# A hybrid decoder step: the first stage by pairs of token tiles

## The chip, the core and the metric

The kernel runs on one core of one Trainium2 chip. The metric is device time in microseconds (us), the median of several runs. A core has a matrix engine (TensorE, PE in the rows, with its weight loads as PEld), a vector engine (VectorE, DVE), an activation engine (ScalarE, ACT), a general engine (GpSimd, POOL) and a queue engine (SyncE, SP) that issues most transfers. Each works through its own instructions in order and waits on semaphores of the others.

## The reference, cut to what matters

One layer is computed for 1024 prompt tokens and for 8 single decode tokens. The first stage, which the change is about, is this:

```python
h = rms_norm(x, norm_g)                      # x: (1024 + 8) x 1024
proj = h @ w_in                              # w_in: 1024 x 3864
b_gate, c_gate, conv_in, z_conv, q, kv, gate_logits, z_attn = split(proj)
q = rope(rms_norm(q, q_gain), pos) * HEAD_DIM ** -0.5      # 8 heads of 64
kv = kv.reshape(bsz, t, 3, 2, 2, 64)         # branch, key or value, head, 64
k = rope(rms_norm(kv[:, :, :, 0], k_gain), pos)
kv_cmp = einsum('bcrjgd,rjde->bcjge', blocks_of_32(kv[branch 0]) + cmp_pe, cmp_w)
```

The second stage is attention in three branches (compressed, selected, window), a short convolution, gates and the output projection; the kernel's diff leaves it alone but for one address.

## The kernel before, in words

All products are made in float32r as three matmuls (high x high, high x low, low x high), so every operand is split: a copy in float32r is the high part, the difference is the low part. For weights this is done by `w_loader`: `fetch` loads a raw piece of two 128-row slices through SP, `split` makes `wh` on ACT and `wl` on POOL.

There are nine token tiles: eight of 128 prompt tokens and one of the 8 decode tokens. In the first stage (`phase0`) a tile of x is loaded (`x_load`, L373), squared and summed on ACT (L382), its root taken in four small DVE steps (`rsqrt`, L194 to L197), scaled on DVE (L384), transposed on PE (L392, `turn_x`) and written as `hH` (ACT) and `hL` (DVE). Then five passes run over the nine tiles, each with 24 matmuls a tile (`tok_mm`, L208 to L210): the keys and values of the compressed, the selected and the window branch, and two halves of Q. Behind each tile follow its norm and rotation on DVE (`norm_rope`, L259 to L275), the output rows and, for keys, doubled rows (`twice`, tile `kd`) that PE transposes one or two tiles later (`cmp_transposes` L408, `k_finish` L489). Such later steps stand in a list `posts`; `posted(n)` runs those that are due, and `posted(9)` flushes it at the end of a pass. Between the selected and the window pass the compression is made (L599).

Beside `phase0` runs `chan_stream`, which makes the same projection with channels on the partitions (`chan_mm`, L223 to L225), in chunks of up to 384 tokens; a first part of it (`z_part`, twelve chunks) is woven into the five passes by `merge`, by weights. The framework lists the instructions in this order, and may move one that it expects to be ready ahead of one that it does not; the order on each engine is then fixed.

PSUM has eight banks: three for matmul results (`mm`), three for transposes (`tp`), two (`cc`) for warm-up matmuls and compression. x has three buffers. `mixC` and `mixA`, outputs of a later stage, lend their memory: `mixC` holds the rope tables, the norm gain as 128 equal rows (`gbc`), and a scratch row. The second rope table's slot is that of `gbc`.

Of the kernel before, what the change touches and what calls it, by code (L numbers as in the profile page):

```python
# [16 lines left out]
D = 1024  # L17
# [43 lines left out]
def hymba_step_kernel(ctx, tc, io):  # L61
    nc = tc.nc
    WARM = 24
# [60 lines left out]
    kv1p = left.enter_context(pool("kv1"))  # L124
    K, V = {}, {}

    K[1] = kv1p.tile([128, 2, 32 + SEQ], F32R, name="k1")
    kpc = K[1][:, :, 0:32]
    KOFF = {1: 32, 2: 0}
    V[1] = kv1p.tile([128, 8, 2, 128], F32R, name="v1")  # L130
# [16 lines left out]
    warm = ps.tile([128, 512], F32, name="cc", tag="cc", bufs=2)  # L147
    for _ in range(WARM):
        PE.matmul(warm[:, :256], vpc[:, 0], vpc.rearrange("p g c -> p (g c)"), start=True, stop=True)

    banks = {"mm": [(ps, "mm", 3)], "tp": [(ps, "tp", 3)], "cc": [(ps, "cc", 2)]}
# [9 lines left out]
    def w_loader(wp, n, kp, raw_bufs, hk, hl_bufs, lo_eng=POOL):  # L161


        def load(col, width):
            hs, ls, raws = [], [], []

            def fetch(i, home=wp):
                r = home.tile([128, kp, n], F32, name="wraw", bufs=raw_bufs)
# [32 lines left out]
    def tok_mm(t, w, n):  # L201

        o = bank("mm")
# [47 lines left out]
    E2 = [(DVE, DVE), (DVE, DVE), (DVE, DVE), (DVE, DVE)]  # L251

    def norm_rope(wk, src, n, t, nh, ct, sn, ea=DVE, eb=DVE):
        w = nh * 64
        sq = wk.tile([128, 256], F32, name="sq")
        ss = wk.tile([128, 8], F32, name="ss", bufs=4)
        if nh == 4:
            ACT.activation(sq[:n, :w], src, AF.Square, scale=0.125)
            DVE.tensor_reduce(ss[:n, :nh], sq[:n, :w].rearrange("p (h d) -> p h d", h=nh), axis=AX, op=OP.add)  # L259
        else:  # L260
            for h in range(nh):
                c = slice(h * 64, h * 64 + 64)
                ACT.activation(sq[:n, c], src[:, c], AF.Square, scale=0.125, accum_out=ss[:n, h:h + 1])
        r = rsqrt(wk, ss[:n, :nh], n, nh)
        qn = wk.tile([128, 4, 64], F32, name="qn")
        q = qn[:n, :nh]
        DVE.tensor_tensor(q, src.rearrange("p (h d) -> p h d", h=nh), r[:, :, None].to_broadcast([n, nh, 64]), OP.mult)
        a = wk.tile([128, 4, 64], F32, name="ra")
        b = wk.tile([128, 4, 64], F32, name="rb")
        ea.tensor_tensor(a[:n, :nh], q, ct[:n, t][:, None, :].to_broadcast([n, nh, 64]), OP.mult)  # L270
        for i in range(2):
            o, s = slice(32 * i, 32 * i + 32), slice(32 - 32 * i, 64 - 32 * i)
            eb.tensor_tensor(b[:n, :nh, o], q[:, :, s],
                               sn[:n, t, o][:, None, :].to_broadcast([n, nh, 32]), OP.mult)
        DVE.tensor_tensor(src.rearrange("p (h d) -> p h d", h=nh), a[:n, :nh], b[:n, :nh], OP.add)  # L275

    def twice(wk, rows, n):

        kd = wk.tile([128, n, 2, 64], F32, name=f"kd{n}", tag="cwr" if n == 4 else "kd2", bufs=CWR if n == 4 else 3)
        v = rows[:, :n * 64].rearrange("p (a d) -> p a d", a=n)  # L280
        copy(DVE, kd, v[:, :, None, :].to_broadcast([128, n, 2, 64]))
        return kd

    def kv_rows(wk, o, t, br, ct, sn):

        if t < 8:
            n, src = 128, o
            rows = wk.tile([128, 256], F32, name="rows", bufs=ROWS)
        else:
            n, src = 8, sum_halves(wk, o, 280 if br == 2 else 256)  # L290
            rows = srows[br] if br else wk.tile([128, 256], F32, name="rows", bufs=ROWS)[:8]
        copy(ACT, rows[:n], src[:n, :256])
        if br == 2:
            copy(ACT, gates[:n, t, :], src[:n, 256:280])
        norm_rope(wk, rows[:n, 0:128], n, t, 2, ct, sn, *E2[br])
        if t == 8:
            if br < 2:
                SP.dma_start(s_rows[br], rows)
            else:
                SP.dma_start(s_win[:, 511, :], rows)  # L300
        elif br < 2:
            SP.dma_start(p_rows[br][t * 128:(t + 1) * 128], rows)
        elif t >= 4:
            SP.dma_start(p_rows[2][(t - 4) * 128:(t - 3) * 128], rows)
        return rows, src


    LAG, DEPTH, HK, HB, XB, ZW, CWR = 1, 2, 2, 4, 3, 43.0, 1
# [6 lines left out]
    def chan_stream():  # L315
# [7 lines left out]
        for p in range(2):  # L323
            nxt[2](p)
# [31 lines left out]
    SM = 0  # L356
    ROWS = 3
    wl0 = w_loader(wk, 280, 2, 2, 1, 10)
    gbc = mCf[:, 2304:3328]

    xcs = ExitStack()
    xcp = xcs.enter_context(pool("xc"))
# [7 lines left out]
    def x_load(t):  # L370
        xts[t] = xsp.tile([128, D], F32, name="xt", bufs=XB)
# [4 lines left out]

    def x_norm(t):
# [3 lines left out]
        ss = wk.tile([128, 1], F32, name="xss", bufs=3)  # L381
        ACT.activation(junk[:n], xt, AF.Square, scale=1.0 / 32, accum_out=ss[:n])  # L382
        r = rsqrt(wk, ss[:n], n, 1)
        DVE.scalar_tensor_tensor(xt, xt, r, gbc[:n], op0=OP.mult, op1=OP.mult)  # L384
# [18 lines left out]
    def cmp_transposes(kd, t):  # L403
# [3 lines left out]
        for a in range(4):  # L407
            PE.transpose(pv[:, a], kd[:, a].rearrange("p r d -> p (r d)"), ident)  # L408
        pp = p.rearrange("p (a c r) -> p a c r", a=4, r=2)
        s = slice(t * 64, t * 64 + 64)  # L410
        for r in range(2):
            q = slice(r * 64, r * 64 + 64)
            copy(ACT, XH[q, :, s], pp[q, :, :, r])
            sub(DVE, XL[q, :, s], pp[q, :, :, r], f(XH[q, :, s]))
# [3 lines left out]
    def cw_fetch(wpool, cw, i):  # L418

        raw = wpool.tile([128, 4, 2, 64], F32, name="cwr", bufs=CWR)  # L420
# [12 lines left out]
    def small_things():  # L433

        cvr = wk.tile([20, 512], F32, name="cvr", tag="cwr", bufs=CWR)
# [3 lines left out]
        SP.dma_start(io["s_conv"].rearrange("l b r c -> (l b) r c")[:, 0, :], state_conv[:, 1, :])  # L439
        p = bank("tp")  # L440
        for i in range(4):
            PE.transpose(p[:, i * 20:i * 20 + 20], cvr[:, i * 128:(i + 1) * 128], ident[:20, :20])
        pv = p[:, :80].rearrange("p (i c) -> p i c", i=4)
        copy(DVE, cvw, pv[:, :, 0:4])
        copy(DVE, stc, pv[:, :, 4:20])

        per = wk.tile([32, 128], F32, name="per", tag="sq")
        SP.dma_start(per, io["cmp_pe"].rearrange("l r j d -> (l r) (j d)"))
        per2 = wk.tile([32, 2, 2, 64], F32, name="per2", tag="qn")
        POOL.tensor_copy(per2, per.rearrange("p (j d) -> p j d", j=2)[:, :, None, :].to_broadcast([32, 2, 2, 64]))  # L450
        p = bank("tp")
# [1073 lines left out]
```

## Time and profile before

| | us |
|---|---|
| median of three runs | 937.73 |
| lowest and highest run | 934.72, 938.48 |
| the profiled execution | 939.33 |
| its span, first to last instruction | 937.6 |

The rows below come from the profiled execution and count from the start of its span. A window's row has its bounds and length, then for each of PE, PEld, DVE, ACT and POOL the busy time with the number of instructions, then the mean granted clock of TensorE (1.00 is 2.4 GHz, 0.50 is 1.2 GHz), the busy share of the DMA engines and GB/s. A row of waits says who waited for whose instruction, the total, how often, and the longest. In a timeline the square bracket is idle time just before, with what ended it; a duration with a count covers all the instructions of the row. Durations of matmuls include the time in the pipe, so their starts tell the pace. L numbers are lines of the kernel.

### The profile page before, as it was taken

How to read it: one execution, taken by the hardware profiler on the slowest of the kernel's cores; microseconds unless marked ns; L12 is line 12 of the kernel's file. 1: busy time of each engine (PE TensorE's matmuls, PEld its weight loads, DVE VectorE, ACT ScalarE, POOL GpSimd, SP SyncE). 2: the span in 40 equal slices, each digit the busy share in tenths (PEclk: the TensorE clock that was granted, in tenths of full speed). 3: DMA queues.
4: the chain of work that ended last, by engine and by line, in shares of the span. 5: the costliest groups of instructions: out<-in, count | busy, mean ns of one | idle time of the engine just before them, and what ended most of it. 6: DMA issues, size and time to landing. Idle time of an engine off the chain costs nothing.

```text
span 937.6 us, 16976 instructions
## 1 busy us (share of the span) xinstructions
PE 873.8 (93%) x5789; PEld 783.2 (84%) x5789; DVE 619.4 (66%) x1714; ACT 556.0 (59%) x1495; POOL 404.3 (43%) x550
## 2 busy tenths in 40 slices
PE   7988999999899999999989999999679999798998
PEld 6888999999689889898979899998568888576765
DVE  5896734788655555856775686577745555877883
ACT  5764543733665655656556666576757666675761
POOL 4132340311454444444434444343455543477761
PEclk8999989999999999999999999999989999899999
DMA  7513331211011000000000100001495661857631
GB/s 246 154 57 95 95 114 35 80 57 31 6 30 34 24 23 24 23 24 23 13 12 23 24 23 1 23 2 44 127 302 182 214 214 47 314 179 226 214 102 47
DMA packets 57955, 82.24 MB, mean 88 GB/s; under 512 B 14470, under 2 KB 43086, under 8 KB 55692
## 3 DMA queue, kind: packets, MB, share of 16 engines
q1 hardware_dynamic: 50956, 47.60, 16.9%
q0 software_dynamic: 6912, 33.56, 10.6%
q8 instruction: 46, 0.75, 0.3%
q14 instruction: 41, 0.34, 0.1%
HBM read 74.24 MB, written 11.10 MB: 91 GB/s over the span
## 4 chain that ended last, share of the span: by engine, by line
PE 49%; ACT 7%; DVE 7%; POOL 3%; issue 3%; DMA 1%; ACTq 0%; DVEq 0%; POOLq 0%
PE o L880 7%; PE pt L870 5%; PE s L796 5%; PE mm L225 5%; PE mm L224 5%; PE mm L223 5%; POOL P L845 2%; ACT P L786 2%; PE mm L1407 1%; PE pt L999 1%; PE mm L1405 1%; PE mm L1406 1%; PE mm L1023 1%; ACT ph L75 1%; PE o L1278 1%
## 5 line engine op out<-in xcount | busy, mean ns | idle before, releaser
L223 PE MATMUL mm<-hH,wh 128*128 128x384 f32 (+1 forms) x480 | 157.9, 329 | 0.0
L225 PE MATMUL mm<-hH,wl 128*128 128x384 f32 (+1 forms) x480 | 155.7, 324 | 0.0
L224 PE MATMUL mm<-hL,wh 128*128 128x384 f32 (+1 forms) x480 | 155.1, 323 | 0.0
L786 ACT ACTIVATE P<-P,stat 128x640 f32<-128x640 f32 (+7 forms) x192 | 112.9, 590 | 37.4 <-DVE stat L784 36.8
L79 POOL TENSOR_TENSOR wl<-wraw,wh 128x256 fp32r<-128x256 f32 (+1 forms) x120 | 87.7, 749 | 106.2 <-ACT wh L75 96.8
L79 DVE TENSOR_TENSOR pl<-pt,ph 128x512 fp32r<-128x512 f32 (+1 forms) x164 | 102.4, 636 | 45.3 <-ACT ph L75 43.9
L75 ACT ACTIVATE ph<-pt 128x512 fp32r<-128x512 f32 (+1 forms) x164 | 88.3, 549 | 66.1 <-PE pt L870 65.5
L845 POOL TENSOR_SCALAR P<-P,stat,gates 128x640 f32<-128x640 f32 (+7 forms) x128 | 101.1, 800 | 55.8 <-DVE stat L836 52.7
L870 PE MATMUL pt<-ident,P 128*128 128x128 f32 x592 | 95.5, 278 | 6.4 <-POOL P L845 3.5
L796 PE MATMUL s<-k,q 128*128 128x320 f32 (+8 forms) x416 | 95.8, 334 | 3.7 <-DVE q L79 1.5
L208 PE MATMUL mm<-wh,hH 128*128 128x256 f32 (+1 forms) x320 | 93.5, 292 | 0.4 <-ACT hH L75 0.4
L209 PE MATMUL mm<-wl,hH 128*128 128x256 f32 (+1 forms) x320 | 93.2, 292 | 0.2
L210 PE MATMUL mm<-wh,hL 128*128 128x256 f32 (+1 forms) x320 | 93.0, 291 | 0.0
L223 PEld LDWEIGHTS mm<-hH,wh 128*128 128x128 f32 x480 | 91.9, 191 | 0.8 <-DVE mixC L693 0.6
L224 PEld LDWEIGHTS mm<-hL,wh 128*128 128x128 f32 x480 | 91.9, 191 | 0.1
L225 PEld LDWEIGHTS mm<-hH,wl 128*128 128x128 f32 x480 | 91.9, 192 | 0.1
L784 DVE CUSTOM_DVE_ANT_0 P<-s,mask 128x32 f32<-128x32 f32 (+8 forms) x160 | 70.9, 473 | 27.0 <-PE s L796 22.4
L870 PEld LDWEIGHTS pt<-ident,P 128*128 128x128 f32 x592 | 70.0, 140 | 19.9 <-POOL P L845 10.1
L880 PE MATMUL o<-ph,v 128*128 128x256 f32 x264 | 74.5, 301 | 3.6 <-ACT ph L75 3.0
L880 PE MATMUL o<-pl,v 128*128 128x256 f32 x264 | 73.3, 300 | 3.3 <-DVE pl L79 3.2
L796 PEld LDWEIGHTS s<-k,q 128*128 128x128 f32 x416 | 66.8, 190 | 8.1 <-DVE q L79 1.7
L841 POOL TENSOR_SCALAR P<-P,stat,gates 128x32 f32<-128x32 f32 x64 | 22.9, 370 | 94.4 <-DVE stat L836 76.4
(342 smaller groups left out, 2182.9 us busy)
## 6 DMA issues: line engine op xcount, KB each, us to landing
wraw<-in_w_in_dram SPq DMA_DIRECT2D x56, 256.0 KB
xt<-in_x_prompt_dram SPq DMA_DIRECT2D x8, 512.0 KB
wor<-in_w_out_dram SPq DMA_DIRECT2D x16, 256.0 KB
xr<-in_x_prompt_dram SPq DMA_DIRECT2D x16, 256.0 KB
out_y_prompt_dram<-xr SPq DMA_DIRECT2D x16, 256.0 KB
sd<-in_state_win_kv_dram SPq DMA_DIRECT2D x8, 512.0 KB
out_s_win_dram<-in_state_win_kv_dram SPq DMA_DIRECT2D x8, 511.0 KB
cwr<-in_cmp_w_dram SPq DMA_DIRECT2D x32, 64.0 KB
```

Of the source, the lines that this page charges most:

```text
L75: return ACT.activation(out, in_, AF.Copy)
L79: return eng.tensor_tensor(out, a, b, OP.subtract)
L208: PE.matmul(o[:, :n], hH[t // 3][:, k, s], wh, start=k == 0, stop=False)
L209: PE.matmul(o[:, :n], hH[t // 3][:, k, s], wl, start=False, stop=False)
L223: PE.matmul(o[:, :n], wh, hH[c][:, k], start=k == 0, stop=False)
L224: PE.matmul(o[:, :n], wh, hL[c][:, k], start=False, stop=False)
L225: PE.matmul(o[:, :n], wl, hH[c][:, k], start=False, stop=k == 7)
L786: return lambda: ACT.activation(P, P, AF.Exp, bias=stt[:, 0, c:c + 1], scale=-1.0, accum_out=stt[:, 1, c:c + 1])
L796: PE.matmul(s[:, a:b], q[:, i], k, start=first, stop=not first)
L845: POOL.tensor_scalar(P[:, i, :n], P[:, i, :n], stt[:, 2, c + i:c + i + 1], gates[:, qi, gt:gt + 1], op0=OP.mult, op1=OP.mult)
L870: PE.transpose(p[:, y * 256 + i * 128:y * 256 + i * 128 + 128], src[:, i], ident)
L880: PE.matmul(o[0][:, :256], v, X[:, y * 256:y * 256 + 256], start=br == 1 and x == 0 and y == 0 and X is h[0], stop=last and y + 1 == len(p ...
```

## The change

- Nine tiles of x have memory of their own (four in `mixA`, five in a pool) and are all loaded early. The memory of the selected branch's keys and values is taken only after that pool is closed.
- The gain is loaded as one row through ACT's queue and spread over the partitions by two matmuls into two PSUM banks (`gps`), from which x is scaled. Warm-up matmuls go from 24 to 8. The banks `cc` are gone.
- `x_stat` takes the roots of two tiles at a time; `x_norm(t + 3)` follows the matmuls of tile t, `turn_x` of tile t + 1 stands right behind the matmuls of tile t (before, that of tile t + 2).
- Two token tiles share a PSUM bank; copy, norm, rotation, value parts and doubled rows are done once for the pair. Squares of keys are summed by a DVE reduction.
- For the compressed branch the doubled rows are replaced by a regrouping of token pairs through four SBUF to SBUF DMAs, so that four transposes serve two tiles, and one ACT copy and one DVE subtraction of 128 partitions replace four of each on 64.
- Later steps wait three tiles instead of one or two, output rows are stored a tile later, and passes no longer flush the list.
- Weights: a third raw buffer, splits at tiles 2 to 6, low parts in turn on POOL and DVE, and 9 buffers for split parts instead of 10. Rope tables are made inside passes.

The diff, cut to its core:

```diff
-    WARM = 24
+    WARM = 8
...
-    banks = {"mm": [(ps, "mm", 3)], "tp": [(ps, "tp", 3)], "cc": [(ps, "cc", 2)]}
+    banks = {"mm": [(ps, "mm", 3)], "tp": [(ps, "tp", 3)]}
...
-                    sub(el, l[:, :, :width], r, f(h[:, :, :width]))
+                    sub(el[j // hk % len(el)] if isinstance(el, tuple) else el, l[:, :, :width], r, f(h[:, :, :width]))
...
-    wl0 = w_loader(wk, 280, 2, 2, 1, 10)
+    wl0 = w_loader(wk, 280, 2, 2, 1, 9)
...
+        xts[t] = mAf[:, t * D:(t + 1) * D] if t < 4 else xsp.tile([128, D], F32, name=f"xt{t}")
...
+    def x_stat(*ts):
+        n = 128 if ts[0] < 8 else 8
+        ss = wk.tile([128, 2], F32, name="xss", bufs=3)
+        for i, t in enumerate(ts):
+            ACT.activation(junk[:n], xts[t][:n], AF.Square, scale=1.0 / 32, accum_out=ss[:n, i:i + 1])
+        r = rsqrt(wk, ss[:n, :len(ts)], n, len(ts))
+        for i, t in enumerate(ts):
+            roots[t] = r[:, i:i + 1]
...
-        DVE.scalar_tensor_tensor(xt, xt, r, gbc[:n], op0=OP.mult, op1=OP.mult)
+        for c in (slice(0, 512), slice(512, D)) if t == 0 else (slice(0, D),):
+            DVE.scalar_tensor_tensor(xt[:, c], xt[:, c], r, gps[:n, c], op0=OP.mult, op1=OP.mult)
...
+    def token_pairs(rows, t):
+        pr = xsp.tile([128, 4, 2, 64], F32, name="pr", bufs=2)
+        for i in range(2):
+            for r in range(2):
+                SP.dma_start(pr[i * 64:i * 64 + 64, :, r], rows[r::2, i * 256:i * 256 + 256].rearrange("p (a d) -> p a d", a=4))
+        return pr
...
+        s = slice(t * 64, t * 64 + 128)
+        copy(ACT, XH[:, :, s], pv)
+        sub(DVE, XL[:, :, s], pv, f(XH[:, :, s]))
...
+            pair.append(tok_mm(t, w, n) if t % 2 == 0 else tok_mm(t, w, n, pair[0][:, 256:512]))
+            if t % 2:
+                o = pair[0]
+                pair[:] = [kv_room(br)]
+                copy(ACT, pair[0][1], o.rearrange("p (i j c) -> p i j c", i=2, j=2))
...
+            posts.append((lambda t=t: k_finish(br, t, kd), 3))
...
     def phase0():
+        ACT.dma_start(g1, io["norm_g"])
         x_load(0)
-        SP.dma_start(gbc, bcast_rows(io["norm_g"], D))
         SP.dma_start(idt, io["c_ident"])
+        for h in range(2):
+            PE.matmul(gps[:, h * 512:h * 512 + 512], one, g1[:, h * 512:h * 512 + 512], start=True, stop=True)
...
         for t in range(NT):
-            if t + 4 < NT:
-                x_load(t + 4)
-            if t + 2 < NT:
-                turns.append(x_norm(t + 2))
-            o = tok_mm(t, c0[0], 256)
+            o = kv_tile_mm(t, c0[0], 256, 0)
             if turns:
                 turns.pop(0)()
+            if t + 3 < NT:
+                turns.append(x_norm(t + 3))
+            if t in (0, 2):
+                x_stat(t + 4, t + 5)
+            elif t == 4:
+                x_stat(8)
             posted(1)
...
+                posts.append((lambda pr=token_pairs(rows, t - 1), t=t: cmp_transposes(pr, t - 1), 3 if t < 7 else 1))
+            if t == 5:
+                tab1 = rope_tables(io["k_gain"][0, 1], 1, 1.0)
+                small_loads()
+            if t in (2, 3, 4, 5):
+                c1[2](t - 2, ACT, EL)
...
-        posted(9)
```

## Rows read from the trace of the kernel before

**Rows 1.** The page: busy time and share of each engine

```profile
PE 873.8 (93%) x5789; PEld 783.2 (84%) x5789; DVE 619.4 (66%) x1714; ACT 556.0 (59%) x1495; POOL 404.3 (43%) x550
```

**Rows 2.** Windows: length; PE, PEld, DVE, ACT, POOL busy; clock; DMA share, GB/s

```profile
8.09:65.73 57.64, 50.28 (x349) 46.72 (x349) 48.53 (x143) 37.78 (x116) 17.13 (x20) 0.91 0.45 143
65.73:111.84 46.11, 42.31 (x319) 41.34 (x319) 32.14 (x119) 22.26 (x91) 16.23 (x23) 0.96 0.35 93
111.84:172.90 61.06, 56.70 (x404) 55.62 (x403) 31.13 (x119) 29.65 (x118) 18.98 (x28) 0.92 0.27 78
172.90:231.80 58.90, 58.90 (x478) 58.59 (x477) 48.87 (x171) 26.67 (x75) 13.49 (x20) 1.00 0.20 57
```

**Rows 3.** Waits of PE, 0 to 232 us: total, times, longest

```profile
PE tp L392 <- DVE xt L384: 5.5, 4, 1.9
PE tp L489 <- DVE kd L76: 3.7, 2, 2.0
PE tp L408 <- DVE kd L76: 3.0, 2, 1.9
PE tp L392 <- DVE rs L194: 2.0, 1, 2.0
```

**Rows 4.** Windows of a few us, columns as in the windows by pass

```profile
20.00:22.00 2.00, 1.93 (x9) 1.96 (x10) 1.30 (x3) 0.60 (x1) 0.00 (x0) 0.50 1.00 372
36.00:38.00 2.00, 1.09 (x10) 1.12 (x11) 2.00 (x12) 0.99 (x2) 0.00 (x0) 1.00 0.14 41
120.00:125.00 5.00, 5.00 (x24) 5.00 (x24) 0.86 (x1) 2.61 (x7) 3.04 (x5) 0.50 0.19 53
```

**Rows 5.** Groups on DVE by shape, 0 to 232 us: busy us, mean ns, idle before

```profile
L79 DVE TENSOR_TENSOR hL<-tp,hH 128x512 fp32r<-128x512 f32 x16 | 10.4, 686 | 2.9 <-ACT hH L75 2.8
L267 DVE TENSOR_TENSOR qn<-rows,rs 128x128 f32<-128x128 f32 x24 | 9.2, 382 | 0.6
L273 DVE TENSOR_TENSOR rb<-qn,mixC 128x64 f32<-128x64 f32 x48 | 9.0, 228 | 0.0
...
L79 DVE TENSOR_TENSOR XL<-tp,XH 64x256 fp32r<-64x256 f32 x16 | 6.7, 418 | 3.8 <-ACT XH L75 3.7
L196 DVE SCALAR_TENSOR_TENSOR rs<-rs 128x2 f32<-128x2 f32 x24 | 6.5, 270 | 0.6
L267 DVE TENSOR_TENSOR qn<-q,rs 128x256 f32<-128x256 f32 x14 | 6.4, 459 | 0.3
...
L76 DVE COPY kd<-rows 128x512 f32<-128x512 f32 x8 | 3.8, 475 | 0.1
```

**Rows 6.** Timeline of the queue SP and of POOL: start, length, what, wait before

```profile
9.80 8.64 SPq L373 DMA_DIRECT2D xt<-in_x_prompt_dram  x2
...
93.97 2.58 SPq L425 DMA_DIRECT2D cwr<-in_cmp_w_dram  x4
...
60.39 2.79 POOL L246 TENSOR_TENSOR mixC<-mixC,g 128x576 f32<-128x576 f32 x2 [28.84 <-DVE xt L384]
64.91 3.05 POOL L79 TENSOR_TENSOR wl<-wraw,wh 128x256 fp32r<-128x256 f32 x4 [1.73 <-PE mm L213]
```

**Rows 7.** Timeline of PE at the start and at the wait for a root

```profile
1.11 5.06 PE L149 MATMUL cc<-vpc 128*128 128x256 f32 x24 [1.11 <-POOL vpc L104]
8.09 1.22 PE L392 MATMUL tp<-ident,xt 128*128 128x128 f32 x8 [1.93 <-DVE xt L384]
...
14.77 0.28 PE L210 MATMUL mm<-wh,hL 128*128 128x256 f32 x1
...
36.91 1.06 PE L392 MATMUL tp<-ident,xt 128*128 128x128 f32 x8 [2.04 <-DVE rs L194]
37.81 0.60 PE L408 MATMUL tp<-ident,kd 128*128 128x128 f32 x4
```

**Rows 8.** Timeline of DVE: one root step alone and one beside POOL

```profile
106.17 0.16 DVE L197 SCALAR_TENSOR_TENSOR rs<-rs 128x2 f32<-128x2 f32 x1
...
113.54 0.70 DVE L197 SCALAR_TENSOR_TENSOR rs<-rs 128x2 f32<-128x2 f32 x1
```

More of the change, by code (lines that the diff above doesn't have):

```diff
@@ L250, in hymba_step_kernel, with norm_rope, room @@
     EC = DVE
[L251 to L270, printed above, removed]
+    def norm_rope(src, n, t, ct, sn):
+        m, nh = src.shape[1:3]
+        def room(name):
+            r = wk.tile([128, 512], F32, name=name)[:n, :m * nh * 64]
+            return r.rearrange("p (i h d) -> p i h d", i=m, h=nh)
+        sq = room("rb")
+        ss = wk.tile([128, 8], F32, name="ss", bufs=4)[:n, :m * nh]
+        ACT.activation(sq, src, AF.Square, scale=0.125)
+        DVE.tensor_reduce(ss, sq.rearrange("p i h d -> p (i h) d"), axis=AX, op=OP.add)
+        r = rsqrt(wk, ss, n, m * nh).rearrange("p (i h) -> p i h", i=m)
+        q = room("qn")
+        DVE.tensor_tensor(q, src, r[:, :, :, None].to_broadcast([n, m, nh, 64]), OP.mult)
+        DVE.tensor_tensor(src, q, ct[:n, t:t + m][:, :, None, :].to_broadcast([n, m, nh, 64]), OP.mult)
+        b = room("rb")
@@ L407, in cmp_transposes, with cw_fetch @@
         for a in range(4):
[L408 to L414, printed above, removed]
+            PE.transpose(pv[:, a], pr[:, a].rearrange("p r d -> p (r d)"), ident)
+        s = slice(t * 64, t * 64 + 128)
+        copy(ACT, XH[:, :, s], pv)
+        sub(DVE, XL[:, :, s], pv, f(XH[:, :, s]))
     cmpw = io["cmp_w"]
-    def cw_fetch(wpool, cw, i):
-        raw = wpool.tile([128, 4, 2, 64], F32, name="cwr", bufs=CWR)
+    def cw_fetch(wpool, cw, i, RB=1):
+        raw = wpool.tile([128, 4, 2, 64], F32, name="cwr", tag="wraw", bufs=RB)
         for r in range(2):
@@ L504, in kv_tile @@
     def kv_tile(t, w, n, br, tab):
[L505 removed]
+        kv_tile_mm(t, w, n, br)
         posted(1)
[L507 to L516 removed]
@@ L518, in q_tile, with kv_tile_rows @@
-    def q_tile(t, w, which, tab):
-        o = tok_mm(t, w, 256)
-        posted(1)
-        src, m = (o, 128) if t < 8 else (sum_halves(wk, o, 256), 8)
-        dst = qt[t] if t < 8 else q_s
-        d = dst[:m, which * 256:which * 256 + 256]
-        copy(ACT, d, src[:m, :256])
-        norm_rope(wk, d, m, t, 4, *tab, *E2[3])
-    qt = []
+        kv_tile_rows(t, br, tab)
+    def kv_tile_rows(t, br, tab):
+        if t % 2 == 0 and t < 8:
+            return None
+        o = pair[0]
+        pair.clear()
+        rows = kv_rows(o, t - t % 2, br, *tab)
+        if t < 8 and br:
+            t -= 1
+            rv = rows[:, 256:512].rearrange("p (i g d) -> p i g d", i=2, g=2)
+            v = V[br][:, t:t + 2]
+            copy(ACT, v[:, :, :, 0:64], rv)
+            sub(POOL, v[:, :, :, 64:128], rv, f(v[:, :, :, 0:64]))
+            kd = wk.tile([128, 4, 2, 64], F32, name="kd2", bufs=2)
+            copy(DVE, kd, rows[:, 0:256].rearrange("p (a d) -> p a d", a=4)[:, :, None, :].to_broadcast([128, 4, 2, 64]))
+            posts.append((lambda t=t: k_finish(br, t, kd), 3))
+        return rows
@@ new lines, in q_tile @@
+    def q_tile(t, w, which, tab):
+        o = tok_mm(t, w, 256) if t % 2 == 0 else tok_mm(t, w, 256, pair[0][:, 256:512])
+        pair.append(o)
+        posted(1)
+        if t % 2 == 0 and t < 8:
+            return
+        o = pair[0]
+        pair.clear()
+        if t < 8:
+            d = qp[t // 2][:, which]
+            copy(ACT, d, o)
+            norm_rope(d.rearrange("p (i h d) -> p i h d", i=2, h=4), 128, t - 1, *tab)
+        else:
+            d = q_s[:, which * 256:which * 256 + 256]
+            copy(ACT, d, sum_halves(wk, o, 256)[:, :256])
+            norm_rope(d.rearrange("p (i h d) -> p i h d", i=1, h=4), 8, 8, *tab)
@@ L575, in phase0 @@
+        cw = cwp.tile([128, 16, 2, 128], F32R, name="cw")
         c2 = wl0(COL_KV + 512, 280)
```

295 lines of the change are left out of this document (159 added, 136 removed).

## Prediction, made before the changed kernel was seen

> **What bounds the kernel now.** I read the page first: its busy line has PE at 93% of the span, with every other engine far below [rows 1]. So time is won only where PE waits or runs slowly. I then cut the first stage, the one that is rewritten, at the ends of its token passes, into four windows [rows 2]: the compressed K/V pass, the selected pass, the block compression with the window pass, and the two Q passes. The stage ends at 231.8 us; after it comes work that the diff touches only in the address from which the doubled queries are read. In each window the reader should compare PE busy with the length, and look at the granted clock. Length minus busy is idle: 7.4, 3.8, 4.4 and 0 us. The clock has two levels, 2.4 and 1.2 GHz, so a mean of 0.91 over 57.64 us means that 0.09 x 57.64 = 5.2 us of full-speed time were lost; likewise 1.8, 4.9 and 0. The excess over gap-free full-speed work is 12.6, 5.6, 9.3 and 0: 27.5 us in all. That is what there is to win. The last window also says what a good pass looks like: no idle and clock 1.00, with DVE busy 48.87 of 58.90.
>
> The waits of PE say where the idle time comes from [rows 3]. Four waits are for a normalized x tile (5.5 us, of which 1.9 lie ahead of the first transposes), one for an x root (2.0), four for the doubled rows (3.7 and 3.0). All end in DVE work that was too late for a transpose that stands fixed in PE's order. Fine windows show what follows: the clock is 0.50 from 20 to 22 and from 120 to 125 us, after such waits, but stays 1.00 after the 2.04 us wait that ends at 36.91 [rows 4, 7]. So an idle stretch may cost twice, not always.
>
> **The change part by part.**
>
> *x loaded at once.* Before, three x buffers hold SP back: two x loads occupy it for 8.64 us [rows 6]. Afterwards nine tiles have their own room and no load waits for a reader. The bytes are the same; this takes away cause, not work: the 2.0 us wait for an x root and the 3.6 us of xt waits past the start go, if DVE keeps up.
>
> *DVE work of the first window* [rows 5]. A tile's norm and rotation now are three 128x128 operations (0.382 at most), two halves (0.228) and four root steps (0.270): 2.7 us. A pair takes three 128x256 operations (0.459), two halves that are 128x128 (at most 0.382), one reduction, new on DVE (0.459 as the nearest), and four root steps: 3.7. Four pairs save 4 x (5.4 - 3.7) = 6.8. Roots of x are taken for two tiles at a time, five times for nine: 4 x 4 x 0.270 = 4.3 saved. The eight doubled rows (0.475) become DMAs: 3.8 saved. Sixteen half subtractions XL (0.418) become four of 128x512 (0.686): 3.9 saved. In all 18.8. Added are four low parts of the next weights (0.459), four high parts of the first channel weights (0.459) and the small tables, some 3 us: 6.7. DVE goes from 48.5 to about 36.5 us [rows 2], below PE's need, which is 57.6 - 12.6 = 45.0, less 14 of the 16 transposes that are dropped at 0.11 each (eight in 0.9 us, 36.91 to 37.81 [rows 7]): 43.4. So PE becomes this window's bound.
>
> *The transposes of x.* The norm now runs two steps ahead, but the transposes of tile t+1 are issued after the matmuls of tile t; before, those of t+2 were. So matmuls of t+1 wait for a round trip: transposes, a copy on ACT, a subtraction on DVE (0.686 for a half [rows 5]). Below, this is nothing, where channel matmuls or later transposes are placed in between; above, it is 0.69 and as much again on ACT, 1.4 us for each of eight tiles, 11 us. I take 3 us, nearer the lower end, since two channel chunks already lie in this window and x is ready earlier.
>
> *Half speed at the start.* Before, the first tile's matmuls end near 15.05 us, and the weights' low parts on POOL set their pace, eight at 0.76 each [rows 6, 7]. These stay on POOL, so the first tile ends as before; I take 0, between -0.6 (x's norm in two halves lets the transposes start half of it earlier) and +1.5 (x's second square now stands in front of the weight copies on ACT, and the gain row must go through PE). The gain row's two matmuls have room: sixteen warm-ups at 5.06 / 24 = 0.21 go, 3.4 us, beside the wait of 1.93 [rows 7]. If their cover went, the first norm would be late by what they exceed 5.3 us. I leave 2 us for half speed. The first window keeps 3 + 2 and, for collisions of DVE with POOL, 1.5 more: 43.4 + 6.5 = 49.9 instead of 57.6. **Gain 7.7**, between 2 (round trip of 11, start +1.5) and 14 (nothing left).
>
> *Pairs by DMA.* Four SP issues for each pair of tiles, 256 KB in pieces of 256 B. The nearest row is a fetch of compression weights, four issues of the same size and pieces: 2.58 us on SP [rows 6]. Behind them on SP stand stores and weight loads, which have a tile or more to spare. The transposes that read them come three steps later, over ten us; only the last pair has one step. Without that cover they cost what they cost now, 1 to 2 us a wait [rows 3].
>
> *The second window.* Leftovers are no longer flushed: the transposes of keys come three steps behind, and the small tables leave this window. That removes the waits on doubled rows. The rope tables too: now POOL stands 28.84 us behind the last x tile, because the tables and the gain share memory, and the next weights' low parts follow only afterwards [rows 6]; afterwards the tables are made at tile 5. What stays is the change of weights: one spare buffer instead of two, so all but one part must wait for the last tile's matmuls. The pace there was POOL's, four in 3.05 us [rows 6]; shared with DVE it is about half of that. I leave 1.5 of 5.6. **Gain 4.1**, between 1 and 5.6.
>
> *The third window.* The same, twice (compression, then Q weights); the fourth raw buffer still frees only when the last tile runs, so some waiting remains. I leave 3 of 9.3. **Gain 6.3**, between 1 and 9.3. POOL and DVE disturb each other here: a root step of 0.16 took 0.70 while POOL subtracted [rows 8]; with half of the low parts moved, POOL's stretches shorten.
>
> *Q passes and what follows:* 0. There is no excess to remove; DVE is 10 us below PE, and pairs lower it. The last pair's chain is 1.0 us longer than a single tile's; attention's first units could start that much later. Bounds +2 and 0.
>
> **Sum.** 7.7 + 4.1 + 6.3 = 18.1. The profiled execution took 939.33 us (span 937.6 and 1.7 around it); 939.33 - 18.1 = 921.2. It lies 1.6 above the median of the runs, so I predict 919.6, about **920**.
>
> **The rivals.**
>
> *All of it goes* (chance 0.13). The Q window shows that a pass can run with no loss. Then 27.5 and 1.6 of transposes are won: 909. Against it: weights still change over at three places.
>
> *Only one kind of wait goes* (0.15). Round trip and DVE keep the first window at 2 us of gain, and the later windows win half their excess, 7.4: 9.4 less, 928. For it: that window's DVE is busy 48.5 of 57.6 us, and operations stretch beside POOL [rows 2, 8].
>
> *Nothing changes* (0.06). Waits move from doubled rows to weights and the pair DMAs, as both stand in the same queues: the time stays near 937. For it: the idle after the selected pass falls together with the weight change [rows 6]. Against it: most of PE's waits name the parts that go.
>
> *Slower* (0.06): the round trip in every tile, with the clock following. Each of eight tiles waits 2.0 us, the size of today's waits, 16 us; and with a wait in every tile half of the 43.4 us of work runs at 1.2 GHz, 21.7 us more. That is 37.7 of loss against 12.6 now: 25.1 more, less 10.4 won later, 14.7: 952. It turns the sign once the window's loss exceeds 12.6 + 10.4 = 23.0, so with 16 us idle from 7 us of work at half speed on. For it: the stretch from 20 us on ran at 0.50 after such waits; against it: the wait at 36.91 left the clock at 1.00 [rows 4, 7]. The Trainium skill, page "TensorE: Matmul & The Clock Gate", section "HAM oscillation — how this bites in real kernels", says that a loop whose bursts of matmuls alternate with waits falls back to the lower clock again and again. By that rule this rival is the likely one as soon as a wait stands in each tile; the trace agrees in two of the three places shown.
>
> **How the numbers follow.** The forecast (0.60) has its own range from 913 to 926: half of each bound. What a measurement of this kernel can tell from no change is about 0.5%, 4.7 us, so "faster" is below 933. Forecast, all and one kind lie below: 0.60 + 0.13 + 0.15, less 0.03 for the upper end of one kind, 0.85; same 0.09; slower 0.06. The range from 909 to 932 leaves out the last two rivals and the far edges of the others.
>
> **What would show it.** Right: windows cut at the ends of the passes of some 50, 42 and 55 us, with the Q window unchanged near 59; no wait of PE over 1 us on doubled rows; SP without a stretch on x; XL in four operations; DVE in the first window under 40 us. Wrong: a PE wait on hH or hL before each tile's matmuls (the round trip); granted clock below 0.9 in the first window; PE waiting on wl at the starts of passes; or an attention stage, from the end of the Q window on, that is not 705.8 us long within 2.

## The result, and the profile after

| | changed kernel | kernel before |
|---|---|---|
| median of 12 runs each, us | 943.73 | 938.65 |
| lowest and highest | 939.44, 949.81 | 934.72, 943.32 |
| ratio of the two, 95% interval | 1.0065 [1.0045, 1.0084] | |
| the profiled execution, its span | 940.05, 938.3 | 939.33, 937.6 |

The change costs 0.65%, some 5 us. 920 was forecast.

The engines first. The busy line on the page of the changed kernel (that of before is in [rows 1]):

```profile
PE 875.8 (93%) x5761; PEld 781.6 (83%) x5761; DVE 596.3 (64%) x1523; ACT 533.9 (57%) x1331; POOL 393.1 (42%) x526
```

All engines but PE have less to do: DVE gave up 23 us. PE has the same work and the span has not moved, so PE's idle and slow time must have stayed the same or changed place. Windows of the changed kernel, cut where the decode tile of the compressed, selected and window pass ends and at the first transposes of the attention:

```profile
7.88:60.76 52.88, 46.92 (x343) 44.50 (x344) 37.58 (x91) 28.66 (x68) 18.16 (x19) 1.00 0.51 167
60.76:105.33 44.57, 40.82 (x306) 40.12 (x306) 30.03 (x92) 16.16 (x40) 12.44 (x15) 0.96 0.32 86
105.33:162.35 57.02, 51.89 (x365) 50.07 (x363) 23.38 (x69) 22.40 (x64) 12.65 (x15) 0.91 0.29 85
162.35:238.70 76.35, 71.35 (x544) 69.27 (x543) 52.91 (x130) 30.17 (x67) 11.37 (x18) 0.98 0.19 51
```

The first two windows of before are in [rows 2]; the last two, cut at the same marks, were these in the kernel before:

```profile
111.84:166.28 54.44, 51.76 (x364) 50.94 (x363) 26.44 (x105) 23.14 (x101) 14.97 (x23) 0.91 0.26 76
166.28:235.79 69.51, 67.83 (x541) 67.23 (x540) 56.98 (x196) 34.42 (x96) 17.50 (x27) 1.00 0.20 57
```

So the compressed pass won 57.64 - 52.88 = 4.8 us and the selected one 46.11 - 44.57 = 1.5; with 0.2 at the start the changed kernel is 6.5 us ahead at 105.33. Then it loses 57.02 - 54.44 = 2.6 on compression and window pass, and 76.35 - 69.51 = 6.8 on Q up to the attention: 2.9 us behind. What follows takes 938.3 - 238.7 = 699.6 us, against 701.8 before.

Who makes PE wait, 0 to 240 us of the changed kernel (before: [rows 3]):

```profile
PE tp L508 <- DVE kd L76: 2.4, 1, 2.4
PE pt L858 <- POOL qd L852: 2.2, 1, 2.2
PE tp L400 <- DVE mixA L392: 1.9, 2, 1.1
PE mm L209 <- POOL wl L79: 1.8, 2, 1.5
PE mm L204 <- ACT hH L75: 1.7, 2, 1.5
PE gps L682 <- DVE cw L79: 1.7, 2, 0.9
PE tp L424 <- DMA pr<-rows: 1.5, 1, 1.5
PE tp L475 <- POOL qn L467: 1.4, 1, 1.4
PE tp L694 <- DVE kc L689: 1.4, 1, 1.4
```

Before, four names held 14.2 of 19 us in this stretch; now the nine shown hold 16 of 22, and the largest is 2.4. The x tiles and doubled rows that the change was about went from 14.2 to 4.3 us. New are weights (`cw`, `wl`), what follows the compression (`kc`), the pairs (`pr`), and `qd`, the first doubled queries of the attention.

The third window is the instructive one. Three timelines of the changed kernel around the compression, first that of ACT, then the queue SP, then DVE:

```profile
107.67 0.61 ACT L75 ACTIVATE cw<-cwr 128x512 fp32r<-128x512 f32 x1
...
116.53 0.63 ACT L75 ACTIVATE cw<-cwr 128x512 fp32r<-128x512 f32 x1 [1.92 <-DMA cwr<-in_cmp_w_dram]
...
126.36 0.27 ACT L75 ACTIVATE vpc<-tp 32x128 fp32r<-32x128 f32 x1 [1.29 <-PE tp L694]
127.40 0.60 ACT L75 ACTIVATE k<-tp 128x512 fp32r<-128x512 f32 x1 [0.78 <-PE tp L508]
127.90 1.71 ACT L75 ACTIVATE wh<-wraw 128x280 fp32r<-128x280 f32 x5
```

```profile
92.08 2.66 SPq L438 DMA_DIRECT2D cwr<-in_cmp_w_dram  x4
...
110.90 0.32 SPq L298 DMA_DIRECT2D out_s_slc_dram<-srows  x1
111.46 3.30 SPq L438 DMA_DIRECT2D cwr<-in_cmp_w_dram  x4
```

```profile
91.37 0.69 DVE L79 TENSOR_TENSOR cw<-cwr,cw 128x512 fp32r<-128x512 f32 x1 [2.57 <-ACT cw L75]
...
109.43 1.40 DVE L269 TENSOR_TENSOR srows<-srows,rb 8x128 f32<-8x128 f32 x1
110.76 0.67 DVE L79 TENSOR_TENSOR cw<-cwr,cw 128x512 fp32r<-128x512 f32 x1
```

The compression's weights come in four raw pieces through one buffer, so a fetch waits until DVE has made the low part of the piece before it: the second low part ends at 92.06 and the third fetch starts at 92.08. The third piece then waits for its place in ACT's order and is split there only at 107.67; its low part on DVE stands behind a rotation that took 1.40 us (POOL was making rope tables from 109.26 on) and ends at 111.43. Only then can SP fetch the fourth piece, at 111.46; a store just ahead of it, which waited for the same rotation, was through at 111.22. The piece reaches ACT at 116.53. By then the compression's results are late, and five of the high parts of the window pass's weights stand in ACT's order behind them, at 127.90. Fine windows of the changed kernel:

```profile
105.00:110.00 5.00, 5.00 (x44) 5.00 (x43) 4.18 (x13) 2.64 (x7) 1.24 (x2) 1.00 0.41 111
110.00:115.00 5.00, 4.19 (x35) 3.98 (x34) 1.43 (x2) 1.71 (x5) 5.00 (x6) 1.00 0.15 34
115.00:120.00 5.00, 3.34 (x27) 2.99 (x25) 1.08 (x4) 1.07 (x3) 0.48 (x1) 1.00 0.96 269
120.00:125.00 5.00, 4.57 (x32) 4.43 (x32) 0.47 (x2) 0.63 (x3) 0.00 (x0) 0.74 0.20 74
125.00:130.00 5.00, 2.77 (x10) 1.90 (x11) 2.85 (x7) 2.54 (x8) 1.60 (x2) 0.50 0.53 157
```

From 115 to 120 DVE, ACT and POOL are busy for 1.1 of 5 us or less and PE for 3.34, while the DMA engines carry the fourth piece and other loads: no engine's work is the bound here. Of PE's 1.66 us of idle time, 0.86 end with the fourth piece's low part and 0.80 with DVE's work on the first half of the compression's result. From 125 to 130 PE is busy 2.77 of 5, at half clock.

In the kernel before, the fourth piece was later still. Its low part on DVE, and the first matmul that uses it:

```profile
130.81 0.69 DVE L79 TENSOR_TENSOR cw<-cwr,cw 128x512 fp32r<-128x512 f32 x1 [7.03 <-ACT cw L75]
```

```profile
131.56 0.31 PE L599 MATMUL cc<-XH,cw 128*128 128x66 f32 x1
```

No wait stands in front of that matmul: 36 matmuls of the window pass, from 126.7 on, lie ahead of it in PE's order and end at 131.6.

### The profile page after: what moved, and what is told of

Read it like the earlier page. It is cut to its first block, busy times and chain, and to the rows that moved or that the text cites. A ratio compares the mean times of both kernels' runs of the same rounds, so it can differ in the third digit from the quotient of the medians.

```text
span 938.3 us, 16573 instructions
## 1 busy us (share of the span) xinstructions
PE 875.8 (93%) x5761; PEld 781.6 (83%) x5761; DVE 596.3 (64%) x1523; ACT 533.9 (57%) x1331; POOL 393.1 (42%) x526
## 3 DMA queue, kind: packets, MB, share of 16 engines
q0 software_dynamic: 6912, 33.56, 10.6%
## 4 chain that ended last, share of the span: by engine, by line
PE 48%; ACT 7%; DVE 7%; POOL 3%; issue 3%; DMA 2%; ACTq 0%; DVEq 0%; POOLq 0%
PE o L970 7%; PE pt L960 6%; PE s L886 5%; PE mm L221 5%; PE mm L220 5%; PE mm L219 5%; POOL P L935 2%; ACT P L876 1%; PE pt L1089 1%; ACT ph L75 1%; PE o L1368 1%; PE om L1113 1%; PE mm L1113 1%; PE mm L1497 1%; PE mm L1496 1%
## 5 line engine op out<-in xcount | busy, mean ns | idle before, releaser
L221 PE MATMUL mm<-hH,wl 128*128 128x384 f32 (+1 forms) x480 | 155.6, 324 | 0.5 <-POOL wl L79 0.5
L79 POOL TENSOR_TENSOR wl<-wraw,wh 128x256 fp32r<-128x256 f32 (+1 forms) x104 | 77.0, 758 | 140.8 <-ACT wh L75 106.0
L935 POOL TENSOR_SCALAR P<-P,stat,gates 128x640 f32<-128x640 f32 (+7 forms) x128 | 100.7, 797 | 56.0 <-DVE stat L926 52.9
L204 PEld LDWEIGHTS mm<-wh,hH 128*128 128x128 f32 x320 | 62.1, 194 | 5.1 <-ACT hH L75 2.7
```

Source lines behind the costliest of these rows:

```text
L79: return eng.tensor_tensor(out, a, b, OP.subtract)
L204: PE.matmul(o[:, :n], hH[t // 3][:, k, s], wh, start=k == 0, stop=False)
L221: PE.matmul(o[:, :n], wl, hH[c][:, k], start=False, stop=k == 7)
L935: POOL.tensor_scalar(P[:, i, :n], P[:, i, :n], stt[:, 2, c + i:c + i + 1], gates[:, qi, gt:gt + 1], op0=OP.mult, op1=OP.mult)
```

## The experiments

**The changed kernel again.**

> The changed kernel itself once more, for a second profile and for the spread of its runs. If the first profile is typical, the third window (compression and window pass) again shows the compression's last matmul near 124 us, a clock of 0.50 behind it, and the stage ends near 232 us; the median stays 3 to 7 us above the kernel before. If the medians differ from the profile by chance of the clock, this profile shows more stretches at 0.50 than the first (mean clock 0.969 to 0.974 instead of 0.976) and a stage that ends up to 8 us later.

944.78 us, ratio 1.0081 [1.0050, 1.0113]. The loss is repeatable. Its profile ends the first stage at 240.2 (first transposes of the attention), so the two profiles of the changed kernel are 2.9 and 4.4 us behind the 235.8 of before, and take 699.6 and 699.9 afterwards.

**Four places for the compression weights, and that with ten buffers for split weights.** Both lend memory of `mixA` to `cw_fetch`.

```diff
-        raw = wpool.tile([128, 4, 2, 64], F32, name="cwr", tag="wraw", bufs=RB)
+        raw = mAf[:, 2064 + 512 * i:2576 + 512 * i].rearrange("p (a j d) -> p a j d", a=4, j=2)
```

The second one makes the split parts `wh` and `wl` ten each and lets a third raw piece of a weight block land in a scratch part of `mixC`:

```diff
-    wl0 = w_loader(wk, 280, 2, 2, 1, 9)
+    wl0 = w_loader(wk, 280, 2, 2, 1, 10)
-                c2[1](2, cwp, 1)
+                c2[1](2, None)
-                nxt[1](2, wx, 1)
+                nxt[1](2, None)
```

> The four raw pieces of the compression weights get four places in the memory of mixA that is not written before 138 us, so that no load waits for the split of the piece before it; all else as in the changed kernel. Theory A (the fourth piece comes late, the compression is late, and the split weights and matmuls that stand behind it in the orders of ACT and PE wait with it): the compression ends 8 us or more earlier, no wait of PE on cw, the stage ends 5 to 8 us earlier, ratio to the kernel before 0.997 to 1.001. Theory B (too few split buffers hold up each change of weights): the waits at 128 and 171 us stay, less than 2 us won, ratio 1.004 to 1.007.

> As the run before, and ten buffers for split parts instead of nine; the third raw piece of the window and Q weights lies in mixC's scratch row. Theory A alone: as the run before, within 1 us. Theory B: the waits for wh and wl at the changes of weights (128 and 171 to 174 us, with 2 us at 0.50 behind each) go, 3 to 5 us more than the run before, ratio 0.992 to 0.997.

942.81 us (1.0039 [1.0011, 1.0067]) and 941.21 (1.0032 [1.0007, 1.0058]). `cw_fetch` is also called late in the second stage, where `mixA` holds results: those two kernels overwrite part of them, so a part of y is computed from other data. The first stage ended earlier in both, at 235.9 and 230.7, but the gain did not come through, and the trace says why. In the first of them, a wait of PE between 630 and 800 us, and ACT's timeline just ahead of it:

```profile
PE pt L1089 <- ACT reg L75: 7.2, 1, 7.2
```

```profile
689.79 0.63 ACT L75 ACTIVATE cw<-mixA 128x512 fp32r<-128x512 f32 x1 [5.41 <-DMA mixA<-in_cmp_w_dram]
690.33 1.13 ACT L75 ACTIVATE reg<-raw 128x512 f32<-128x512 f32 x2
```

ACT stands 5.41 us in front of a piece that may land in `mixA` only after POOL has written there, and `reg`, for which PE waits, is next in its order. In the changed kernel this wait is 1.3. That was the edit's own doing, so both were made again for the first stage alone.

**One tile of x transposed ahead of the first pass**, a rival's cause: the round trip of the transposes.

```diff
+        turns.pop(0)()
         for t in range(NT):
             o = kv_tile_mm(t, c0[0], 256, 0)
```

> The transposes of x again two tiles ahead of the matmuls, as in the kernel before: tile 1 is transposed ahead of the first pass; all else as in the changed kernel. Theory C (the round trip of transposes, copy and subtraction costs in each tile of the first pass): the first window's idle of 6.0 us falls to 3 or less and the pass ends 2 to 4 us earlier, ratio 1.002 to 1.004. Rival: x's turn is covered by channel matmuls and later transposes already, the window is bound by weights at the start and pairs at 41 us: under 1 us, ratio 1.005 to 1.008.

946.51 us, 1.0073 [1.0049, 1.0098]. The first pass ends at 55.9 instead of 60.8: with the round trip nearly all of its idle time behind the start goes, the wait for the pairs (1.5) among it. The pass won more than theory C expected, and yet the median is the rival's. At once PE waits 2.3 us for position rows that POOL copies late (`qn`), and later 4.6 for `cw` (1.7 in the changed kernel). Nothing is left of the 5 us at the end of the stage (239.6).

**The two buffers again, each alone and both, lent only to the first stage; and nine buffers in the kernel before.**

```diff
-        raw = wpool.tile([128, 4, 2, 64], F32, name="cwr", tag="wraw", bufs=RB)
+        if lent:
+            raw = mAf[:, 2064 + 512 * i:2576 + 512 * i].rearrange("p (a j d) -> p a j d", a=4, j=2)
+        else:
+            raw = wpool.tile([128, 4, 2, 64], F32, name="cwr", tag="wraw", bufs=RB)
```

The tenth buffer is made as above; the kernel before gets `w_loader(wk, 280, 2, 2, 1, 9)`.

> The changed kernel, but the four pieces of the first stage's compression weights land in four places of their own (memory that held tiles 2 and 3 of x, which is free by then); the later stage fetches as the changed kernel does. Theory A (the first stage's gain is given back because the weights of the compression and of the window pass come late, piece after piece through one buffer): the compression's own transposes stand at about 119 us instead of 126, the first stage ends 3 to 4 us earlier and, the 702 us behind it unchanged, the median falls from 944 to about 940.5. Rival B (what is lost lies behind the first stage, or in waits that only change their name): the first stage may end earlier, but the median stays within 1 us of 944.

> The changed kernel with ten instead of nine buffers for the high and low parts of the first stage's weights, paid for by letting the third raw piece of a weight block land in scratch memory; the compression weights still come one piece at a time, through one place. A: the tenth buffer alone lets the window pass and the Q passes have their first weights split one step sooner, at the three weight changes; the first stage ends 3 to 5 us earlier (the two experiments that changed both together ended it 8 to 9.5 us earlier, the pieces apart alone 3 to 4), median about 940. If the two only work together: below 1 us, median 943 to 944. B: within 1 us of 944.

> Both edits of the two kernels before it: four places for the first stage's compression weights, ten buffers for the high and low parts; the later stage is untouched. A: the first stage ends about 8 us earlier than in the changed kernel (first transposes behind it at about 231), with 702 us behind it: a span of 933 and a median of about 935, faster than the kernel before. B: the later stage waits for what does not move with it (the wait ahead of the regrouped cache rows, 6 to 7 us in the two earlier versions) and the median stays at 941 or above.

> The kernel before with nine instead of ten buffers for the high and low parts of the first stage's weights, nothing else: one part of the change alone. A: the tenth buffer was worth something before as well: each of three weight changes loses about 1 us, median 940 to 942 against 938. B: no difference beyond 1 us.

Four places: 938.32, ratio 0.9998 [0.9972, 1.0023]. Ten buffers: 941.47, 1.0040 [1.0022, 1.0058]. Both: 937.49, 0.9999 [0.9973, 1.0024]. Nine buffers in the kernel before: 946.83, 1.0108 [1.0081, 1.0135]. So the late pieces alone are worth the whole loss, 5.4 us: theory A, with 940.5 expected. Ten buffers bring 2.3 and both together 6.2, less than expected. And the ninth buffer, one digit in the diff, costs 8.7 us in the kernel before, more than either expectation and at least as much as the whole change. How, is seen in the profile of that last kernel, in PE's waits, DVE's timeline and POOL's:

```profile
PE tp L611 <- ACT sq L263: 3.3, 1, 3.3
```

```profile
131.24 1.40 DVE L270 TENSOR_TENSOR ra<-qn,mixC 128x128 f32<-128x128 f32 x1
132.56 1.84 DVE L273 TENSOR_TENSOR rb<-qn,mixC 128x64 f32<-128x64 f32 x2
...
134.83 0.23 DVE L604 TENSOR_TENSOR kc<-cc,kc 128x66 f32<-128x66 f32 x1
```

```profile
131.08 2.83 POOL L246 TENSOR_TENSOR mixC<-mixC,g 128x576 f32<-128x576 f32 x2 [6.34 <-DVE g L243]
```

The same operations in the kernel before, with ten buffers, POOL's and then DVE's:

```profile
117.52 2.88 POOL L246 TENSOR_TENSOR mixC<-mixC,g 128x576 f32<-128x576 f32 x2 [3.29 <-DVE ra L270]
```

```profile
132.81 0.29 DVE L270 TENSOR_TENSOR ra<-qn,mixC 128x128 f32<-128x128 f32 x1
133.02 0.35 DVE L273 TENSOR_TENSOR rb<-qn,mixC 128x64 f32<-128x64 f32 x2
```

One buffer fewer moves the tables from 117.52 to 131.08: the last of their gain rows leaves SP at 127.09 instead of 100.98, as it stands behind loads of weights. There the tables lie beside a rotation on DVE, in front of the compression's results: it takes 1.40 us, and 1.84 for the next two operations, instead of 0.29 and 0.35. PE waits 3.3 us instead of 0.7, for `kc`, which DVE finishes at 136.50 (the row names an operation of ACT that ended at the same moment), and runs at half speed from then to about 143. The Trainium skill, page "SBUF — State Buffer", section "SBUF: two separate sides", says that a VectorE operation with two SBUF inputs and a GpSimd operation that reads SBUF hold one shared pair of ports in turn, the other fully blocked; the two rows agree, as the stretched operations begin while POOL is at its tables. That makes most of the 5.0 us by which the stretch of compression and window pass is longer; another 1.8 lie behind it, at the change to the Q weights, where PE stops for `wh` and `wl` piece by piece (0.9 in all). This profile, 943.56 us, is the fastest of its six runs; what the others lose beyond it was not seen.

**A bank apart, and the three moves together.** In the kernel with both buffers the second half of the compression's matmuls waited 1.9 us for vector work on the first half's result, as both halves lie in one two-bank tile, and the clock was 0.50 for 12 us.

```diff
-            o = gps[:, j * 512:j * 512 + 512]
+            o = bank("mm") if j else gps[:, 0:512]
```

The last kernel adds the tile transposed ahead, the doubling of the position rows on DVE one tile earlier in a place of its own, and GpSimd alone for the low parts of the second Q weights:

```diff
+            if t == 6:
+                per2 = mAf[:32, 3840:4096].rearrange("p (j r d) -> p j r d", j=2, r=2)
+                copy(DVE, per2, small_in["per"].rearrange("p (j d) -> p j d", j=2)[:, :, None, :].to_broadcast([32, 2, 2, 64]))
-                        nxt[2](t - 2, ACT, EL)
+                        nxt[2](t - 2, ACT, POOL)
```

The third run has the two moves in the first pass alone, on the changed kernel.

> The changed kernel with four places for the first stage's compression weights and ten buffers for the high and low parts (as in the run that had both, 937.5 us), and the second half of the compression's matmuls in a bank of its own instead of the second half of the two-bank tile. In that run PE waited 1.9 us between the two halves, for vector work on the first half's result, and then ran 8 us at half clock, 105 to 117 us. A: with a bank apart the wait goes, the clock stays up, and the first stage ends at about 226 instead of 231; median 932 to 934. Rival: PE reaches the second half before something else is there (the window pass's weights), the wait moves and the median stays within 1 us of 937.5.

> The kernel with both buffers and the bank apart, and three more moves in the first stage: one tile of x is transposed ahead of the first pass (which took away nearly all of the first pass's idle time, 55.9 instead of 60.8 us, when it was done alone), the position rows are doubled earlier, by the vector engine and in a place of their own (PE had then waited 2.3 us for them and dropped to half clock), and the low parts of the second Q weights are made by GpSimd alone (a wait of 2.2 us at 190). If the first stage's idle time is what the total is made of: it ends at about 219 to 222, and with 702 us behind it the median is 924 to 928. Rival B (the later stage takes back what comes earlier): not under 932.

> The changed kernel with two edits in the first pass alone: one tile of x is transposed ahead of it, and the position rows are doubled earlier, by the vector engine in a place of their own. Buffers and the fetch of the compression weights stay as in the changed kernel. Theory A (what comes late in the third window decides): the first pass ends at about 56 instead of 60.8, the second one 5 us earlier too, and nearly all of it is lost again ahead of the window pass, as its weights cannot come earlier; median 941 to 944. Rival: the first pass's order was the loss, the 5 us go through to the end, median 939.

> The kernel before once more, for a second profile of it. If what differs between executions lies behind the first stage, the first stage ends within 0.5 us of 235.8 (the first transposes behind it) and the rest differs; otherwise the first stage varies as well, and its ends have to be compared with that in mind.

A bank apart: 935.29, 0.9963 [0.9943, 0.9983], between its two expectations and not clear of the kernel without it. From the end of its selected pass (105.0) to the attention it needs 126.2 us, where the kernel with one tile needs 130.2; its stage ends no earlier all the same, as in this execution the compressed pass lost 4 us, at clock 0.66 from 40 to 50. The clock inside the compression did not stay up as expected (last section). All: **927.19, 0.9872 [0.9844, 0.9899]**, faster than both kernels by 11 and 17 us. The median is the expected one, but in part by luck: its stage was to end at 219 to 222 and ends at 225.6. The first pass alone: 940.60, 1.0022 [1.0005, 1.0038]. The kernel before again: first stage to 236.2, 698.1 after it, so what varies between its executions, 3.7 us, lies behind the first stage.

The run of the first pass alone is the clearest test of the theory. Its windows, cut at the same marks, and PE's largest wait:

```profile
7.88:56.87 48.99, 47.00 (x345) 45.50 (x346) 36.68 (x97) 27.88 (x66) 14.82 (x18) 1.00 0.54 177
56.87:96.58 39.71, 38.72 (x305) 38.33 (x304) 27.14 (x76) 15.31 (x39) 10.84 (x13) 1.00 0.38 97
96.58:162.33 65.75, 56.58 (x364) 54.65 (x363) 27.14 (x74) 19.24 (x62) 13.38 (x16) 0.82 0.25 74
162.33:237.49 75.16, 69.89 (x546) 67.59 (x543) 53.63 (x136) 31.34 (x70) 14.17 (x18) 1.00 0.18 52
```

```profile
PE gps L686 <- DVE cw L79: 5.7, 2, 3.3
```

It reaches the compression at 96.58, 8.7 us ahead of the changed kernel and 15.3 ahead of the kernel before, and leaves the window pass at 162.33, where the changed kernel does (162.35). The whole gain is turned into waits, above all for the compression's weights (idle 9.2 us instead of 5.1), and into half-speed work (clock 0.82 instead of 0.91). This execution, 944.86 us, is the slowest of twelve; in the median, 940.60, 3.1 us of the 8.7 are kept. The kernel with everything, at the same marks, keeps it:

```profile
7.88:56.93 49.05, 46.99 (x345) 45.52 (x346) 36.69 (x98) 28.43 (x67) 15.15 (x18) 1.00 0.55 176
56.93:100.52 43.59, 41.75 (x305) 41.32 (x303) 26.50 (x77) 16.56 (x42) 10.77 (x13) 0.92 0.41 111
100.52:153.15 52.63, 51.47 (x364) 50.78 (x363) 25.05 (x73) 18.10 (x59) 12.70 (x16) 0.90 0.23 71
153.15:225.57 72.42, 68.94 (x545) 67.73 (x543) 54.50 (x131) 33.08 (x72) 17.11 (x22) 1.00 0.19 58
```

Ends of the passes, read from PE's timelines (last decode matmul of the selected pass and of the window pass, first transposes of the attention), with the time of the profiled execution that they belong to and the medians. The two kernels that lent the places to the later stage as well are left out.

| kernel | selected | window | stage | profiled | median |
|---|---|---|---|---|---|
| before, two profiles | 111.8, 112.1 | 166.3, 166.6 | 235.8, 236.2 | 939.3, 936.1 | 938 to 939 |
| changed, two profiles | 105.3, 106.7 | 162.4, 163.9 | 238.7, 240.2 | 940.1, 942.8 | 943.7, 944.8 |
| before, nine buffers | 110.4 | 169.8 | 241.1 | 943.6 | 946.8 |
| one tile of x ahead | 99.9 | 164.5 | 239.6 | 946.9 | 946.5 |
| first pass alone | 96.6 | 162.3 | 237.5 | 944.9 | 940.6 |
| four places | 105.4 | 158.0 | 234.4 | 935.3 | 938.3 |
| ten buffers | 101.0 | 158.2 | 232.0 | 936.1 | 941.5 |
| both | 100.7 | 155.6 | 230.9 | 936.2 | 937.5 |
| both, bank apart | 105.0 | 157.5 | 231.2 | 936.0 | 935.3 |
| all | 100.5 | 153.2 | 225.6 | 929.4 | 927.2 |

Within its own execution what follows the stage takes between 698.1 and 705.4 us, so differences of a few us between two profiles can lie there. Some profiles are far from their medians: that of ten buffers is the fastest of its nine runs, that of the first pass alone the slowest of twelve.

## Why the prediction was wrong, point by point

- *What there is to win*, 27.5 us in the first stage: the frame was right. The last kernel ends the stage 10 us earlier than the kernel before.
- *The compressed pass*, gain 7.7: right mechanism, 4.8 measured. DVE has 37.58 us (36.5 forecast), XL is four operations, no x load holds SP, the clock in the row is 1.00. The start, put at 0 between -0.6 and +1.5, cost 2.9: the first tile's matmuls end at 17.99 instead of 15.05, as PE waits 1.46 for `hH` and 1.11 for the second tile of x, whose first transposes stand ahead of the third matmul in PE's order. The round trip, put at 3 us, cost 4 to 5: one tile more in advance took the end of the pass to 55.9, and to 56.9 in the run of the first pass alone.
- *Pairs by DMA*: 2.7 to 3.1 us on SP for four issues (2.58 assumed), one wait of 1.5. Right in price. The cover was shorter than the ten us assumed: the wait is that of the first pair, whose transposes at 40.75 stand 5.7 us behind its first issue.
- *The selected pass*, gain 4.1: 1.5. Doubled rows still made PE wait 2.4 once, and the position rows 1.4.
- *The third window*, gain 6.3: **the step that failed.** It counted the waits that would go and left 3 us for "some waiting". It never followed the compression's weights: four pieces through one buffer, each fetch behind the low part of the piece before it, each split behind other work on ACT and DVE. Their supply has a pace of its own, and in the kernel before it was slow too, the low part of its fourth piece being made at 130.81; but there 36 matmuls of the window pass stood in front of that piece, so PE did not wait. In the changed kernel PE arrives earlier and the piece not as much earlier, and the difference is waiting. The prediction ended this window at 172.90, behind the change to the Q weights, the windows above end it ahead of that. Measured together with Q, so that the mark does not matter, the time from the end of the selected pass to the end of the last Q matmul (231.93 before, 232.35 after) is 127.0 us instead of 120.1: 6.9 lost instead of 6.3 won, 2.6 of it up to the end of the window pass.
- *Q*, 0 within +2: 4.3 lost up to the last Q matmul. At the change of weights PE waits 0.8 for ACT's copy out of a bank and 1.5 for `wl` after 171, with a mean clock of 0.88 from 168 to 182 (1.7 us); the tenth buffer took 1.0 to 2.6 us out of the stretch up to the attention (73.8 and 75.3 instead of 76.4). The prediction had the ninth buffer's price at this change inside the third window's 3 us ("the same, twice"). The last pair's longer chain adds the wait of 2.2 for `qd` behind the Q passes, where the bound was 2.
- *After the Q passes*: 706.0 us against 705.7 before; in the second profiles 706.2 against 702.0, so the kernel before itself varies by more than the 2 us of the test. Right; the wait for `qd` is made good behind it.
- *Rivals.* "Nothing changes", with its reason that waits move from doubled rows to weights, had the cause, though not the size (937); it got 0.06. The loss, 5.1 us, lies just beyond the 4.7 from which the prediction would speak of "slower", also 0.06. But that rival was tied to the round trip in every tile with half speed behind it: in the first pass PE waited for `hH`, `hL` or `hS` four times, 2.7 us in all, and its row has clock 1.00 (but see the last section on its start). As a mechanism it is refuted.
- Open: the means of the two profiled executions of each kernel differ by 3.7 us, the ends of their first stages by 3.5, the medians by 5 to 6.5. Where the slower executions of the changed kernel lose the rest was not seen. Nor was the last kernel's gain split among its three moves.

## What to carry to other kernels

When a stage gets faster, ask of each input of the *next* stage when it can be there at the earliest, following its buffer, its queue and its splits; if that moment does not move as far, the gain ends there. A buffer given up to pay for something else can cost more than the thing brings: price it by taking it away in the old kernel, and by giving it back in the new one, as the price depends on what else it moves (8.7 us here in the old, 2.3 in the new). And free the supply before the consumer: the same two moves in the first pass brought 3 us on their own, and stand in the kernel that brought 17.

## What the runs showed of the hardware

The clock can fall while PE waits for nothing. In the kernel with the bank apart the wait inside the compression is gone, and still:

```profile
107.00:109.00 2.00, 2.00 (x21) 2.00 (x20) 1.97 (x5) 0.00 (x0) 0.35 (x1) 1.00 0.00 0
109.00:111.00 2.00, 2.00 (x19) 2.00 (x19) 1.15 (x4) 0.72 (x2) 0.00 (x0) 0.94 0.48 139
111.00:113.00 2.00, 2.00 (x12) 2.00 (x11) 1.53 (x11) 0.74 (x3) 0.12 (x1) 0.50 0.00 0
```

The rows have PE busy without a gap from 103 to 115 us, and yet the granted clock goes from 1.00 to 0.50 at about 111, among 64 matmuls with 66 columns each, and stays there until 121. In the kernel with everything it falls at about 106.6, among the same matmuls and again without a wait. The prediction took half speed for what follows a wait; the expectation that this edit would keep the clock up fell for the same reason. Busy time includes the time in the pipe, though: the starts of these matmuls lie 0.11 us apart, those of 256 columns ahead of them 0.12, so the rows do not show how much of that time the array itself was at work. The Trainium skill, page "TensorE: Matmul & The Clock Gate", section "What's actually happening", ties the lower clock to an idle engine; these rows show it with PE busy in every slice, and whether that is against the page stays open.

A granted clock of 1.00 in a window is not proof of full speed either. In the first pass of the changed kernel, whose row has 1.00:

```profile
14.99 0.41 PE L204 MATMUL mm<-wh,hH 128*128 128x256 f32 x1
15.20 0.41 PE L205 MATMUL mm<-wl,hH 128*128 128x256 f32 x1
```

From 14.35 to 16.48 the matmuls of 256 columns start 0.21 us apart, as in the kernel before from 10.6 to 11.2, where the clock is 0.50; behind that it is 0.12. By an estimate from these ten intervals, 1 us of the first pass is lost to half speed that the row does not show.
